# A batched x·yᵀ on one core: two heads per 128-row matmul, transposes on the vector engine, stores in 16 KB runs

## The chip, the core and the metric

The kernel runs on one NeuronCore of a Trainium2 chip. The core has a matrix engine (PE, with weight loads listed apart as PEld), a vector engine (DVE), an activation engine (ACT), a general engine (POOL) and a queue engine (SP). Sixteen DMA engines move data between the chip's DRAM and the on-chip SBUF, which has 128 partitions. Matmul results land in PSUM[...]. The metric is the device time of one execution in microseconds.

## The reference

```python
def setup_inputs():
    batch, n_heads, seq_t, seq_s, channels = 8, 12, 512, 512, 64
    # x, y: float32, (8, 12, 512, 64)

def reference(x, y):
    return np.einsum('bhtc,bhsc->bhts', x, y).astype(np.float32)
```

For each of the 96 heads, a 512x64 matrix is multiplied with the transpose of another one. The inputs are 25.17 MB together, the output is 100.66 MB, so four fifths of all bytes are stores.

## The kernel before

The 96 heads are handled in 12 groups (`NG`) of 8. A group is two halves `a` of G = 4 heads. In one half a partition holds R = 16 consecutive rows of one head (4 KB), and a head covers Q = 32 partitions. `load(g)` (L55, L56) brings y and x of a group to SBUF, one DMA of 1 MB each, in 4 KB runs, three groups ahead (`AHEAD`).

A matmul contracts over partitions, so both operands are needed with the 64 channels on partitions. `prepare(g)` makes them, as a generator that the main loop advances step by step, so that preparing the next group is spread over the matmuls of the running one. POOL casts y and x to bf16 (L73), in four instructions of 128x1024 elements. PE transposes 128x128 blocks by matmuls with an identity matrix (L82 for y, L95 for x), 32 per group, into PSUM tiles `pt`; DVE and ACT copy these to `yT` (L88, L90) and `xT` (L100, L102). Since two halves lie side by side in a block, channels of half 0 end on partitions 0 to 63 and those of half 1 on 64 to 127.

In the main loop a result tile `pm` (128 rows, two times 512 columns of fp32) is made by eight matmuls (L122), each with a weight tile of 64 rows and 32 columns, one head's 32 rows. ACT (L129) and DVE (L131) evict such tiles in turn into `ot`, which holds 32 KB per partition; `ot` has three buffers. A full `ot` is one store of 4 MB in 32 KB runs (L136). Only the first and the last half are stored in four pieces of 1 MB, in 8 KB runs (L134). All loads and stores are issued by SP on one queue; the order of the program text is the order of the queue.

Of the kernel before, what the change touches and what calls it, by code (L numbers as in the profile page):

```python
# [1 line left out]

# [5 lines left out]


@with_exitstack  # L10
def kernel(
    ctx: ExitStack,
    tc: tile.TileContext,
    x: bass.AP,
    y: bass.AP,
    out: bass.AP,
):

    nc = tc.nc
    B, H, T, C = x.shape
    _, _, S, _ = y.shape
    P = 128
    G = 4
    Q = P // G
    R = T // Q
    NG = B * H // (2 * G)  # L30
    K = R // 2
    AHEAD = 3
    fp32 = mybir.dt.float32
    bf16 = mybir.dt.bfloat16
    COPY = mybir.ActivationFunctionType.Copy
    assert C * 2 == P and S == T and R == 16

    xv = x.rearrange("b h t c -> (b h t c)").rearrange("(g a p n) -> g p a n", a=2, p=P, n=R * C)
    yv = y.rearrange("b h t c -> (b h t c)").rearrange("(g a p n) -> g p a n", a=2, p=P, n=R * C)
    ov = out.rearrange("b h t s -> (b h t s)").rearrange("(g a p n) -> g a p n", a=2, p=P, n=R * S)  # L40

    const = ctx.enter_context(tc.tile_pool(name="const", bufs=1))
    lpool = ctx.enter_context(tc.tile_pool(name="lpool", bufs=AHEAD))
    bpool = ctx.enter_context(tc.tile_pool(name="bpool", bufs=2))
    tpool = ctx.enter_context(tc.tile_pool(name="tpool", bufs=2))
    opool = ctx.enter_context(tc.tile_pool(name="opool", bufs=3))
    ptpool = ctx.enter_context(tc.tile_pool(name="ptpsum", bufs=2, space=bass.MemoryType.PSUM))
    pmpool = ctx.enter_context(tc.tile_pool(name="pmpsum", bufs=3, space=bass.MemoryType.PSUM))

    loaded = {}  # L50

    def load(g):
        xs = lpool.tile([P, 2, R, C], fp32)
        ys = lpool.tile([P, 2, R, C], fp32)
        nc.sync.dma_start(ys.rearrange("p a r c -> p a (r c)"), yv[g])  # L55
        nc.sync.dma_start(xs.rearrange("p a r c -> p a (r c)"), xv[g])  # L56
        loaded[g] = (xs, ys)

    for g in range(AHEAD):
        load(g)  # L60

    ident = const.tile([P, P], bf16)
    make_identity(nc, ident)

    def prepare(g, made):

        xs, ys = loaded.pop(g)
        yb = bpool.tile([P, R, 2, C], bf16)
        xb = bpool.tile([P, R, 2, C], bf16)
        for s, b in ((ys, yb), (xs, xb)):  # L70
            for half in range(2):
                rows = slice(half * K, (half + 1) * K)
                nc.gpsimd.tensor_copy(b[:, rows], s[:, :, rows].rearrange("p a r c -> p r a c"))  # L73
        if g + AHEAD < NG:
            load(g + AHEAD)
        yield
        yT = tpool.tile([P, G * Q, R], bf16)
        xT = tpool.tile([P, R, P], bf16)
        for half in range(2):
            pt = ptpool.tile([P, K, P], bf16)  # L80
            for k in range(K):
                nc.tensor.transpose(  # L82
                    pt[:, k, :], yb[:, half * K + k].rearrange("p a c -> p (a c)"), ident
                )
            dst = yT[:, :, half * K:(half + 1) * K]
            src = pt.rearrange("p k n -> p n k")
            if half == 0:
                nc.vector.tensor_copy(dst, src)  # L88
            else:
                nc.scalar.activation(dst, src, COPY)  # L90
            yield
        for half in range(2):
            pt = ptpool.tile([P, K, P], bf16)
            for k in range(K):
                nc.tensor.transpose(  # L95
                    pt[:, k, :], xb[:, half * K + k].rearrange("p a c -> p (a c)"), ident
                )
            dst = xT[:, half * K:(half + 1) * K]
            if half == 0:
                nc.vector.tensor_copy(dst, pt)  # L100
            else:
                nc.scalar.activation(dst, pt, COPY)  # L102
            yield
        made[g] = (xT, yT.rearrange("p n k -> p (n k)"))

    made = {}
    for _ in prepare(0, made):
        pass
    for g in range(NG):
        xT, yT = made.pop(g)  # L110
        steps = prepare(g + 1, made) if g + 1 < NG else iter(())
        for a in range(2):
            ot = opool.tile([P, R, S], fp32)
            otf = ot.rearrange("p r s -> p (r s)")
            edge = (g == 0 and a == 0) or (g == NG - 1 and a == 1)
            for k in range(K):
                if k in (0, 3, 6):
                    next(steps, None)
                pm = pmpool.tile([P, 2, S], fp32)
                for two in range(2):  # L120
                    for h in range(G):
                        nc.tensor.matmul(  # L122
                            pm[h * Q:(h + 1) * Q, two, :],
                            xT[a * C:(a + 1) * C, 2 * k + two, h * Q:(h + 1) * Q],
                            yT[a * C:(a + 1) * C, h * S:(h + 1) * S],
                            start=True, stop=True,
                        )
                if k % 2 == 0:
                    nc.scalar.activation(ot[:, 2 * k:2 * k + 2, :], pm, COPY)  # L129
                else:  # L130
                    nc.vector.tensor_copy(ot[:, 2 * k:2 * k + 2, :], pm)  # L131
                if edge and k % 2 == 1:
                    i, j = (2 * k - 2) * S, (2 * k + 2) * S
                    nc.sync.dma_start(ov[g, a][:, i:j], otf[:, i:j])  # L134
            if not edge:
                nc.sync.dma_start(ov[g, a], otf)  # L136


# [1 line left out]
_INS = ['x', 'y']  # L140
_OUTS = [((8, 12, 512, 512), 'float32')]


# [23 lines left out]
```

## Time and profile before

| | before |
|---|---|
| median of 9 runs | 307.4 us (307.31 to 307.54) |
| the profiled execution's own time | 307.42 us |
| its span, first to last instruction | 305.7 us |
| instructions in the span | 4378 |
| PE busy | 204.6 us, 1920 matmuls and 1920 weight loads |
| DVE busy | 138.6 us |
| ACT busy | 119.7 us |
| POOL busy | 49.4 us |
| DMA moved | 126.11 MB, mean 413 GB/s |
| mean granted PE clock | 0.629 of full speed |

The busy times are sums over the span and overlap. A row of the groups table reads: line, engine, operation, output <- input with shapes, count; then total busy time and mean ns of one; then the idle time just before these instructions and what ended most of it. The row "SPq ... <- ..." of the waits table reads: total wait in us, how often, longest. In the slices of the span each digit is a busy share in tenths of one fortieth of the span, here 7.6 us. In a table by stretches the share of DMA is the mean over 16 engines, and packets are booked where they start, so that a short stretch can show more than 1. The trace also has a record of every DMA packet with its start, its duration and its size, though not the engine that moved it.

### The profile page before, as it was taken

Reading aid. Unit: us, or ns where it says so; the run is one execution under the profiler, and the core shown is the slowest. Engines: PE = TensorE matmul, PEld = TensorE weight load, DVE = VectorE, ACT = ScalarE, POOL = GpSimd, SP = SyncE. Lnnn points to the kernel's source line nnn. Section 1 sums busy time; section 2 is a strip of 40 time slices with the busy share of each in tenths; the row PEclk is TensorE's granted clock in tenths of the full one; section 3 lists DMA queues with packets and bytes.
Section 4 is the critical chain, followed back from the end, with each engine's and each line's share of the span. In section 5 each row is a group of like instructions: output and inputs, shape, how many; then the busy total and the mean of one; then the engine's idle time right before and its main releaser. Section 6 shows DMA issues by size and latency. Waiting matters only on the chain.

```text
span 305.7 us, 4378 instructions
## 1 busy us (share of the span) xinstructions
PE 204.6 (67%) x1920; PEld 91.8 (30%) x1920; DVE 138.6 (45%) x120; ACT 119.7 (39%) x121; POOL 49.4 (16%) x54
## 2 busy tenths in 40 slices
PE   1899999979919928926933990991785976575000
PEld 1443234535304403502511530350251432222000
DVE  0465654657416607615633741670664664446000
ACT  1445527544423606605523441560653463325000
POOL 3754024300500500320140050041000000000000
PEclk9999999955555555755675555575575555555555
DMA  7999999999998999999999999999999999999980
GB/s 277 413 409 420 460 419 403 470 418 384 437 467 380 443 437 408 448 425 427 442 423 425 423 441 430 402 458 425 425 440 429 427 437 435 429 429 440 397 370 35
DMA packets 10867, 126.11 MB, mean 413 GB/s; under 512 B 864, under 2 KB 864, under 8 KB 7008
## 3 DMA queue, kind: packets, MB, share of 16 engines
q1 hardware_dynamic: 10848, 125.83, 97.1%
q8 instruction: 15, 0.25, 0.3%
q14 instruction: 4, 0.03, 0.0%
HBM read 25.17 MB, written 100.66 MB: 412 GB/s over the span
## 4 chain that ended last, share of the span: by engine, by line
DMA 49%; PE 29%; DVE 5%; issue 4%; ACT 3%; POOL 1%; SPq 0%; ACTq 0%
DMA out_dram<-ot 47%; PE pm L122 23%; DVE ot L131 5%; PE pt L95 4%; ACT ot L129 3%; DMA xs<-in_x_dram 2%; PE pt L82 2%; POOL xb L73 1%; ACT xT L102 0%; DVE xT L100 0%; SPq L55 0%; ACTq L129 0%; SPq L136 0%
## 5 line engine op out<-in xcount | busy, mean ns | idle before, releaser
L122 PE MATMUL pm<-yT,xT 64*32 64x512 bf16 x1536 | 160.2, 590 | 66.4 <-ACT ot L129 63.8
L131 DVE COPY ot<-pm 128x1024 f32<-128x1024 f32 x96 | 117.1, 1224 | 122.9 <-DMA out_dram<-ot 64.0
L129 ACT ACTIVATE ot<-pm 128x1024 f32<-128x1024 f32 x96 | 96.0, 1023 | 115.5 <-DMA out_dram<-ot 72.0
L122 PEld LDWEIGHTS <-xT 64*32 64x32 bf16 x1536 | 53.6, 119 | 147.8 <-issue 136.0
L73 POOL CAST yb<-ys 128x1024 bf16<-128x1024 f32 x24 | 24.3, 1042 | 143.6 <-DMA ys<-in_y_dram 68.5
L82 PE MATMUL pt<-ident,yb 128*128 128x128 bf16 x192 | 24.0, 297 | 8.6 <-POOL yb L73 6.8
L102 ACT ACTIVATE xT<-pt 128x1024 bf16<-128x1024 bf16 x12 | 12.3, 1024 | 37.0 <-PE pt L95 30.2
L95 PE MATMUL pt<-ident,xb 128*128 128x128 bf16 x192 | 25.8, 310 | 1.3 <-DVE xT L100 0.8
L73 POOL CAST xb<-xs 128x1024 bf16<-128x1024 f32 x24 | 24.3, 1042 | 13.6 <-issue 4.9
L95 PEld LDWEIGHTS <-xb 128*128 128x128 bf16 x192 | 19.4, 142 | 22.7 <-issue 20.0
L82 PEld LDWEIGHTS <-yb 128*128 128x128 bf16 x192 | 19.3, 138 | 17.8 <-issue 8.2
L88 DVE COPY yT<-pt 128x1024 bf16<-128x1024 bf16 x12 | 14.6, 1216 | 8.5 <-PE pt L82 8.5
L90 ACT ACTIVATE yT<-pt 128x1024 bf16<-128x1024 bf16 x12 | 12.2, 1019 | 8.3 <-PE pt L82 8.3
L100 DVE COPY xT<-pt 128x1024 bf16<-128x1024 bf16 x12 | 8.3, 690 | 12.2 <-PE pt L95 9.7
L90 ACT ACT_TABLE_LOAD x1 | 1.3, 1283 | 0.7 <-PEq L151 0.7
masks.py:199 POOL TENSOR_SCALAR_AFFINE_SELECT ident<-ident 128x128 bf16<-128x128 bf16 x1 | 0.3, 294 | 0.1
masks.py:197 POOL MEMSET ident<- 128x128 bf16 x1 | 0.2, 205 | 0.3 <-POOLq L151 0.3
L151 POOL MEMSET const-float32-0.0<- 128x1 f32 x1 | 0.1, 99 | 0.2 <-issue 0.2
L151 POOL MEMSET const-bfloat16-1.0<- 128x1 bf16 x1 | 0.1, 102 | 0.0
L151 POOL MEMSET const-uint8-127<- 128x1 uint8 x1 | 0.1, 102 | 0.0
L151 POOL MEMSET const-float32-1.0<- 128x1 f32 x1 | 0.1, 99 | 0.0
## 6 DMA issues: line engine op xcount, KB each, us to landing
out_dram<-ot SPq DMA_DIRECT2D x22, 4096.0 KB, 27.7
ys<-in_y_dram SPq DMA_DIRECT2D x12, 1024.0 KB, 21.0
xs<-in_x_dram SPq DMA_DIRECT2D x12, 1024.0 KB, 23.1
out_dram<-ot SPq DMA_DIRECT2D x8, 1024.0 KB, 19.1
```

The costliest lines, as they stand in the source:

```text
L73: nc.gpsimd.tensor_copy(b[:, rows], s[:, :, rows].rearrange("p a r c -> p r a c"))
L82: nc.tensor.transpose(pt[:, k, :], yb[:, half * K + k].rearrange("p a c -> p (a c)"), ident)
L88: nc.vector.tensor_copy(dst, src)
L90: nc.scalar.activation(dst, src, COPY)
L95: nc.tensor.transpose(pt[:, k, :], xb[:, half * K + k].rearrange("p a c -> p (a c)"), ident)
L100: nc.vector.tensor_copy(dst, pt)
L102: nc.scalar.activation(dst, pt, COPY)
L122: nc.tensor.matmul(pm[h * Q:(h + 1) * Q, two, :], xT[a * C:(a + 1) * C, 2 * k + two, h * Q:(h + 1) * Q], yT[a * C:(a + 1) * C, h * S:(h + ...
L129: nc.scalar.activation(ot[:, 2 * k:2 * k + 2, :], pm, COPY)
L131: nc.vector.tensor_copy(ot[:, 2 * k:2 * k + 2, :], pm)
L151: nc = _bacc.Bacc("TRN2", target_bir_lowering=False, num_devices=1)
```

## The change

The groups stay at 8 heads, but a head now covers 16 partitions with R = 32 rows each, so a load is one run of 8 KB per partition. There is no half `a` any more: a group is worked in two halves of four heads (partitions 0 to 63, and 64 to 127), and each half in two results `h` of two heads.

The transposes leave PE. POOL casts x with four instructions of 32 partitions and y with two of 64 (L70). Each moves one half of the channels (32) to other partitions. For x, the value goes into one 16-bit slot of a 32-bit word, slot `u`, on the partitions of head pair member `u`; the other slot stays zero (the tiles `zeroed` are cleared once). For y, two neighbouring rows are packed into one word. DVE then transposes 32x32 blocks of 32-bit words (L102, L107), two instructions per half of a group, straight into SBUF. The transposed x has, on 128 partitions (channel half, `u`, channel), columns in which the rows of two heads alternate; where a column belongs to the other head, the partition holds zeros.

So one matmul with a full 128x128 weight tile gives 64 rows each of two heads (L123), 384 in all. ACT evicts three of four tiles (L128) and DVE the third (L126). `ot` holds 16 KB per partition and has seven buffers; a store is 2 MB: 64 runs of 16 KB in each of two heads (L129). No store is split at the edges. The order of instructions is the program's (`manual_schedule`), with `prepare` reduced to casts at steps 0 and 1, transposes at 5 and 13, and the load of a later group at 12. For the first group, DVE and ACT share the casts.

```diff
-    G = 4
+    G = 8
...
-    NG = B * H // (2 * G)
-    K = R // 2
+    NG = B * H // G
+    K = 8
+    E = R // K
+    D = 32
...
+    ov = out.rearrange("b h t s -> (b h t s)").rearrange(
+        "(o u h q n) -> o h q u n", u=2, h=2, q=Q * E, n=K * S
+    )
...
-    bpool = ctx.enter_context(tc.tile_pool(name="bpool", bufs=2))
-    tpool = ctx.enter_context(tc.tile_pool(name="tpool", bufs=2))
-    opool = ctx.enter_context(tc.tile_pool(name="opool", bufs=3))
-    ptpool = ctx.enter_context(tc.tile_pool(name="ptpsum", bufs=2, space=bass.MemoryType.PSUM))
-    pmpool = ctx.enter_context(tc.tile_pool(name="pmpsum", bufs=3, space=bass.MemoryType.PSUM))
+    ybpool = ctx.enter_context(tc.tile_pool(name="ybpool", bufs=2))
+    tpool = ctx.enter_context(tc.tile_pool(name="tpool", bufs=4))
+    opool = ctx.enter_context(tc.tile_pool(name="opool", bufs=7))
+    pmpool = ctx.enter_context(tc.tile_pool(name="pmpsum", bufs=4, space=bass.MemoryType.PSUM))
...
+    zeroed = [const.tile([P, K * E * D], u32, name=f"xb{half}") for half in range(2)]
...
+    def casts(g, half, engines):
...
+        xb = zeroed[half]
+        xv2 = xb.bitcast(bf16).rearrange("p (k e c u) -> p k e c u", k=K, e=E, u=2)
+        base = half * 64
...
+        for ch in range(2):
+            for u in range(2):
+                lo = base + u * D
+                src = xs[lo:lo + D, :, ch * D:(ch + 1) * D]
+                cast(
+                    engines[n % len(engines)],
+                    xv2[(2 * ch + u) * D:(2 * ch + u + 1) * D, :, :, :, u],
+                    src.rearrange("p (e k) c -> p k e c", k=K),
+                )
+                n += 1
+        yb = ybpool.tile([P, R // 2 * D], u32)
+        yv2 = yb.bitcast(bf16).rearrange("p (j c w) -> p j w c", j=R // 2, w=2)
+        for ch in range(2):
+            cast(
+                engines[n % len(engines)],
+                yv2[ch * 64:(ch + 1) * 64],
+                ys[base:base + 64, :, ch * D:(ch + 1) * D].rearrange("p (j w) c -> p j w c", w=2),
+            )
+            n += 1
...
+    def transposes(g, half, xb, yb):
+        xT = tpool.tile([P, K * D * E], u32)
+        nc.vector.transpose(
+            xT.rearrange("p (k r e) -> p k e r", k=K, e=E),
+            xb.rearrange("p (k e c) -> p k e c", k=K, e=E),
+        )
+        yT = tpool.tile([P, D * R // 2], u32)
+        nc.vector.transpose(
+            yT.rearrange("p (r j) -> p j r", r=D), yb.rearrange("p (j c) -> p j c", c=D)
+        )
...
+    def result(g, half, h, steps):
...
+        ot = opool.tile([P, K, S], fp32)
+        for k in range(0, K, 2):
+            next(steps, None)
+            pm = pmpool.tile([P, 2, S], fp32)
+            for two in range(2):
+                nc.tensor.matmul(
+                    pm[:, two, :], xT[:, k + two, h, :], yT[:, h * S:(h + 1) * S], start=True, stop=True
+                )
+            if k == 4:
+                nc.vector.tensor_copy(ot[:, k:k + 2, :], pm)
+            else:
+                nc.scalar.activation(ot[:, k:k + 2, :], pm, COPY)
+        nc.sync.dma_start(ov[2 * g + half, h], ot.rearrange("p r s -> p (r s)"))
+
+    def prepare(g):
...
+        for step in range(16):
+            if step in (0, 1):
+                b[step] = casts(g, step, [nc.gpsimd])
+            if step in (5, 13):
+                transposes(g, step // 8, *b[step // 8])
+            if step == 12 and g + AHEAD < NG:
+                load(g + AHEAD)
+            yield
+
+    with tc.manual_schedule():
+        for g in range(AHEAD):
+            load(g)
+        nc.vector.memset(zeroed[0], 0.0)
+        nc.gpsimd.memset(zeroed[1], 0.0)
+        b0 = casts(0, 0, [nc.vector, nc.scalar, nc.gpsimd])
+        transposes(0, 0, *b0)
+        b1 = casts(0, 1, [nc.gpsimd, nc.scalar])
+        transposes(0, 1, *b1)
+        if AHEAD < NG:
+            load(AHEAD)
+        for g in range(NG):
+            steps = prepare(g + 1) if g + 1 < NG else iter(())
             for half in range(2):
...
+                for h in range(2):
+                    result(g, half, h, steps)
```

## The prediction

> **What bounds the kernel now.** I read the page's slices of the span first, then its table of DMA queues, then the issuing queue's waits, then busy time in chosen stretches, and last the groups of instructions. Each time below is of the one profiled execution: span 305.7 us, time 307.42 us, against a median of 307.4 us, so the two can be used for each other.
>
> ```profile
> DMA  7999999999998999999999999999999999999980
> GB/s 277 413 409 420 460 419 403 470 418 384 437 467 380 443 437 408 448 425 427 442 423 425 423 441 430 402 458 425 425 440 429 427 437 435 429 429 440 397 370 35
> ...
> q1 hardware_dynamic: 10848, 125.83, 97.1%
> q8 instruction: 15, 0.25, 0.3%
> ```
>
> The reader is to see that the 16 DMA engines are busy in every slice but the first and the last two; one queue moves all 125.83 MB in 97.1% of the engines' span. No compute engine passes 67% on the page.
>
> ```profile
> SPq L136 <- DVE ot L131: 231.8, 22, 15.2
> SPq L162 <- DMA out_dram<-ot: 22.0, 3, 17.2
> ...
> L131 DVE COPY ot<-pm 128x1024 f32<-128x1024 f32 x96 | 117.1, 1224 | 122.9 <-DMA out_dram<-ot 64.0
> L129 ACT ACTIVATE ot<-pm 128x1024 f32<-128x1024 f32 x96 | 96.0, 1023 | 115.5 <-DMA out_dram<-ot 72.0
> L73 POOL CAST xb<-xs 128x1024 bf16<-128x1024 f32 x24 | 24.3, 1042 | 13.6 <-issue 4.9
> ```
>
> SP (L136) waits for evictions, but the evictions (L129, L131) wait 72.0 and 64.0 us for stores to leave `ot`: compute is ahead and held by full buffers. At the end the program waits 22.0 us for stores alone. So a faster or slower engine is worth nothing until it falls under the DMA pace; what counts is how long the **last** DMA engine takes. Busy time by stretches (columns: length, then PE, PEld, DVE, ACT, POOL busy with counts, PE clock, DMA share, GB/s):
>
> ```profile
> 109.00:114.00 5.00, 0.00 (x0) 0.00 (x0) 0.00 (x0) 0.00 (x0) 0.00 (x0) 0.50 0.97 419
> 115.00:124.00 9.00, 8.48 (x79) 3.81 (x79) 5.91 (x6) 4.34 (x5) 0.00 (x0) 0.50 0.94 397
> 160.00:250.00 90.00, 61.38 (x588) 28.69 (x591) 43.89 (x39) 38.06 (x39) 8.11 (x8) 0.54 1.01 431
> 292.00:295.00 3.00, 0.00 (x0) 0.00 (x0) 0.00 (x0) 0.00 (x0) 0.00 (x0) 0.50 1.01 429
> 300.00:304.00 4.00, 0.00 (x0) 0.00 (x0) 0.00 (x0) 0.00 (x0) 0.00 (x0) 0.50 0.06 27
> ```
>
> The last line carries the prediction: for 4 us the DMA share is 0.06, one engine of 16, moving 27 GB/s. Fifteen engines are done and the kernel waits for one. The trace's DMA packet records (start, duration, size; no engine number) say why. A 32 KB store packet takes 1213 ns, in 2,636 of 2,816 cases exactly; 118 take 1231 to 1316 ns, 7.38 us too much in all, and they follow one another as packets of one engine do. From 109 to 114 us, with no instruction on any engine, all 52 are at 1213 or 1214 ns. From 115 to 124 us, with 173 instructions, there is one chain of slow ones (1255, 1288, 1265, 1293 ns and so on). After 282.3 us, when compute has ended, none is slow. So one DMA engine loses time while instructions run: 2,802 instructions ran during the 118 packets, 2.6 ns each. The last packet ends at 304.27 us; the other 15 engines end from 295.6 to 299.8, mean 297.6.
>
> [...]
>
> **The change, part by part.**
>
> *Packets.* Fixed sizes in the records: 4 KB 159 ns, 8 KB 309, 32 KB 1213, nearly a straight line; 16 KB lies at 309 + 8192 x (1213-309)/24576 = 610 ns. Per engine before: 384 loads x 159 + 64 edge stores x 309 + 176 stores x 1213 = 294.3 us. After: 24 loads x 8 packets x 309 = 59.3, and 48 stores x 8 x 610 = 234.2, together 293.6 us. The 18 more semaphore packets of 9 ns each are 0.2. Gain about 0.5 us.
>
> *Instructions.* 1,536 matmuls with as many weight loads and 384 transposes with theirs go; 384 matmuls with 384 loads come. PE falls from 3,840 to 768 instructions; with some 99 on DVE, 150 on ACT, 143 on POOL, 72 on SP, the program has about 1,250 against 4,378. The 15 instruction fetches (q8; 14.9 us of packets by the records, 0.9 us per engine on average) should fall to about 4: gain 0.6 us. The slow engine's loss was 304.27 - 297.6 = 6.7 us over 4,378 instructions, 1.5 ns each; at 1,250 it is 1.9 us. From the other side, 2.6 ns each gives 3.3; below, the loss can vanish, and then the others' spread (up to 2.2 us over their mean, less with fewer fetches, say 1.5) ends last. I take 1.9.
>
> *Sum.* Mean end of the engines: first packet at 1.9, 293.8 of packets, and of the 1.4 us by which 297.6 exceeded 1.9 + 294.3 the 0.8 that isn't fetches: 296.5. With 1.9 of lag, 298.4. From the last packet to the reported time were 307.42 - 304.27 = 3.15 us. That makes **301.5 us**.
>
> *Compute beside it.* A group of 8 heads has 293.6/12 = 24.5 us of DMA. In it: ACT 12 x 1.023 = 12.3 us; DVE 4 x 1.224 for evictions and two pairs of transposes. Their price is not in the trace[...]. PE: the page's matmuls of 512 columns last 590 ns on average, so 32 of them one after another are at most 18.9 us. POOL: 12 casts; the trace has 1.042 us for 128x1024, and 32 or 64 partitions with as many elements each take the same if cost goes by elements: 12.5 us. All lie under 24.5 and cost nothing; the cover is 7 `ot` tiles of 2 MB, 34 us of stores, against 3 of 4 MB. New waits: a transpose waits on POOL with DVE's evictions behind it, ACT then gets three PSUM tiles further at most before PE is held too (4 in all); this eats only into that 34 us backlog. SP's loads for three groups on stand behind three stores of the running group and wait for casts that were queued eleven steps earlier.
>
> *Start.* x lands at about 5.7 us and y at 8.2, as y and x did. ACT and POOL then have six and five casts between them, to about 12.6; transposes 1, matmuls, and ACT's three evictions put the first store at about 16. Loads of three groups fill the queue to 16.9 us and the fourth, issued at 12.6 when the casts free its tiles, to 22. No gap; with casts twice as long about 2 us of one.
>
> **Rivals.** (1) *The lag stays*: one engine is slow because evictions or stores run, not by number of instructions. For it: the slow packets come with all engines' work, which the trace can't part. Against: 2.6 ns for each instruction is steady, and PE has 88% of them. Then 296.5 + 6.7 + 3.15 = 306.3 us.
>
> (2) *POOL becomes the bound, slower than before.* The casts write every second bf16 and change partitions. [...] the 1042 ns with permuted rows speak against. It decides from 24.5/12 = 2.04 us per cast. [...]
>
> (3) *16 KB stores to two heads 1 MB x 2 apart run under the line.* 384 packets per engine: 16 ns too many on each eat the gain; at 650 ns the time is 317. Against: three sizes lie on one line.
>
> **How the numbers follow.** Forecast 0.66, own range 299.6 (no lag at all: 296.5 + 3.15) to 303.5 (3.3 us of lag and a small gap at the start). Rival 1 0.15, 305.6 to 307.4; POOL 0.08; stores 0.06; a gap of several us at the start or in the middle 0.05. The range for 8 in 10 runs from 299.4 to 306.6 and takes in most of rival 1. About 0.2%, 0.6 us, is what this kernel's measurement tells from no change: faster is below 306.8. Faster 0.66 + 0.11 + 0.04 = 0.81, same 0.05, slower 0.14.
>
> **What would show it.** Right: the stretch in which one engine works alone shrinks from about 4 us to under 2, GB/s near 428 from 20 us on, the final wait for stores ends near 300 us of span, evictions still wait for stores. Wrong: a lone engine for 4 us or more (rival 1); POOL busy over 80% and SP waiting for evictions that wait for transposes (rival 2); DMA share 9 in every slice at under 420 GB/s (rival 3). The forecast fails as soon as DMA slices drop below 9 in the middle.

## The result and the profile after

The changed kernel takes 305.0 us (median of 9 runs, 304.62 to 305.37) against 307.41 us (28 runs): a ratio of 0.9921, interval 0.9912 to 0.9929. It is faster by 2.4 us, or 0.8%, where 5.9 us were forecast. Its profiled execution took 304.83 us.

From the page of the changed kernel: span, busy times, the DMA slices, the queues, and groups.

```profile
span 303.0 us, 1551 instructions
...
PE 135.3 (45%) x384; PEld 46.2 (15%) x384; DVE 131.0 (43%) x99; ACT 144.9 (48%) x150; POOL 182.4 (60%) x142
...
DMA  7999999999999999999999999999999999999992
GB/s 294 428 376 439 415 435 424 439 421 423 438 410 427 441 416 432 435 420 432 426 433 407 430 430 423 427 433 421 425 441 425 430 426 433 428 437 425 437 428 115
...
q1 hardware_dynamic: 10368, 125.83, 98.0%
q8 instruction: 3, 0.05, 0.1%
...
L128 ACT ACTIVATE ot<-pm 128x1024 f32<-128x1024 f32 x144 | 136.8, 1028 | 120.5 <-DMA out_dram<-ot 99.8
...
L70 POOL CAST xb<-xs 32x1024 bf16<-32x1024 f32 x91 | 120.6, 1325 | 49.7 <-DMA xs<-in_x_dram 30.6
L126 DVE COPY ot<-pm 128x1024 f32<-128x1024 f32 x48 | 58.1, 1215 | 114.6 <-DMA out_dram<-ot 108.3
...
L102 DVE STREAM_TRANSPOSE xT<-xb 128x1024 uint32<-128x1024 uint32 x24 | 49.6, 2066 | 13.2 <-POOL xb L70 11.7
L107 DVE STREAM_TRANSPOSE yT<-yb 128x512 uint32<-128x512 uint32 x24 | 25.0, 1041 | 6.2 <-POOL yb L70 6.2
```

The reader is to see that nothing has changed about the bound. The DMA slices are full from the second to the last but one. Evictions, the copies of `pm` to `ot`, still wait for stores (99.8 us on ACT, 108.3 on DVE; it was 72.0 and 64.0), so compute is further ahead than before. Instructions fell from 4378 to 1551, instruction fetches (q8) from 15 to 3. Busy time by stretches of the changed kernel (columns as in the table of before):

```profile
160.00:250.00 90.00, 44.99 (x121) 14.99 (x120) 41.19 (x32) 42.88 (x46) 47.83 (x37) 0.67 1.01 427
...
294.00:296.00 2.00, 0.00 (x0) 0.00 (x0) 0.00 (x0) 0.00 (x0) 0.00 (x0) 0.50 1.01 434
296.00:298.00 2.00, 0.00 (x0) 0.00 (x0) 0.00 (x0) 0.00 (x0) 0.00 (x0) 0.50 0.40 172
298.00:300.00 2.00, 0.00 (x0) 0.00 (x0) 0.00 (x0) 0.00 (x0) 0.00 (x0) 0.50 0.27 115
300.00:302.00 2.00, 0.00 (x0) 0.00 (x0) 0.00 (x0) 0.00 (x0) 0.00 (x0) 0.50 0.04 16
```

The steady rate is as before (427 GB/s, 431 then). The end looks different. Before, one engine of 16 worked alone for 4 us; now a share of 0.27 from 298 to 300 us says that four or five engines work, and one alone only for the last 1.1 us. The trace also records when each of the 16 engines signals that its part of a DMA has landed (sixteen times for each DMA, without engine numbers). For the last store, in us from the span's start, sorted:

```
before  295.9 296.0 296.0 296.0 296.4 296.8 296.8 297.5 298.6 298.7 298.7 298.8 299.1 299.3 300.1 304.7
after   296.5 296.5 296.5 296.6 296.7 296.8 296.8 297.0 297.2 297.5 298.1 299.5 299.9 300.3 301.0 302.1
```

| last store's signals, us | before | after | forecast for after |
|---|---|---|---|
| last of 16 | 304.69 | 302.12 | 298.8 |
| mean of 16 | 298.10 | 298.07 | 296.9 |
| last over mean | 6.59 | 4.05 | 1.9 |

(The forecast counted packets' ends, which lie 0.4 us before the signal for the last one: 304.27 and 304.69 before.) So 2.5 us came from the lateness of the last engine, and nothing from the mean. Of the 3.3 us by which the profiled execution missed the forecast, 2.1 are lateness and 1.2 mean. (The forecast's mean was that of the fifteen other engines; taken so, after has a mean of 297.8 and a lateness of 4.3, and the parts are 2.4 and 0.9.)

What makes engines late in the changed kernel is read from the same signals of all DMAs: the last engine's lead over the median stands still for long and jumps at some DMAs. From 62 to 89 us it stays at 1.2 to 1.5 us and is 2.2 at 94; it goes from 3.2 to 4.3 at 170 us and from 4.4 to 5.3 at 219 us. These jumps fall on loads. (An earlier one, at 62 us, falls on one of the three instruction fetches, 0.92 us long.) The packet records agree: after 20 us, 74 of 2,156 load packets of 8 KB are more than 105 ns too long (up to 931 ns in place of 309), in bunches around the loads that stand between stores. Their excess over 309 ns sums to 22.1 us. From 5 to 20 us, where only loads run, none of 780 is. In the kernel before, the 4 KB load packets after 20 us had 8.4 us of excess.

The packet records carry no engine number, but they can be strung together by time: on one engine a packet starts 3 to 4 ns before the recorded end of the packet before it, and all 16 engines work through the same order of packet sizes. (Where two engines end within a nanosecond or two of each other, they can be taken for one another, so the sums by engine are good to some tenths of a us.) Read so, the engine that ends last in the changed kernel has 4.5 us of excess in its load packets, 0.4 us in its stores and one fetch; of the ten engines that end first, none has over 1.6 us in its loads. In the kernel before, the last engine has 7.8 us of excess in its 32 KB stores and no fetch on q8 at all.

### The profile page after: what moved, and what is told of

It reads as the page before. It is cut to its first block, busy times and chain, and to the rows that moved or that the text cites. A ratio compares the mean times of both kernels' runs of the same rounds, so it can differ in the third digit from the quotient of the medians.

```text
span 303.0 us, 1551 instructions
## 1 busy us (share of the span) xinstructions
PE 135.3 (45%) x384; PEld 46.2 (15%) x384; DVE 131.0 (43%) x99; ACT 144.9 (48%) x150; POOL 182.4 (60%) x142
## 4 chain that ended last, share of the span: by engine, by line
DMA 75%; POOL 10%; ACT 2%; issue 1%; DVE 0%; ACTq 0%; PE 0%; SPq 0%; POOLq 0%
DMA out_dram<-ot 63%; DMA ys<-in_y_dram 12%; POOL xb L70 6%; POOL yb L70 4%; ACT ot L128 2%; DVE ot L126 0%; ACTq L186 0%; PE pm L122 0%; SPq L62 0%; POOLq L70 0%; ACTq L128 0%; SPq L129 0%; DVE yT L107 0%; SPq L63 0%
## 5 line engine op out<-in xcount | busy, mean ns | idle before, releaser
L128 ACT ACTIVATE ot<-pm 128x1024 f32<-128x1024 f32 x144 | 136.8, 1028 | 120.5 <-DMA out_dram<-ot 99.8
L122 PE MATMUL pm<-yT,xT 128*128 128x512 bf16 x384 | 135.3, 504 | 131.5 <-ACT ot L128 96.7
L70 POOL CAST xb<-xs 32x1024 bf16<-32x1024 f32 x91 | 120.6, 1325 | 49.7 <-DMA xs<-in_x_dram 30.6
L126 DVE COPY ot<-pm 128x1024 f32<-128x1024 f32 x48 | 58.1, 1215 | 114.6 <-DMA out_dram<-ot 108.3
L122 PEld LDWEIGHTS <-xT 128*128 128x128 bf16 x384 | 46.2, 120 | 220.1 <-issue 194.9
L70 POOL CAST yb<-ys 64x1024 bf16<-64x1024 f32 x46 | 60.7, 1319 | 3.3 <-DMA ys<-in_y_dram 0.5
L102 DVE STREAM_TRANSPOSE xT<-xb 128x1024 uint32<-128x1024 uint32 x24 | 49.6, 2066 | 13.2 <-POOL xb L70 11.7
L107 DVE STREAM_TRANSPOSE yT<-yb 128x512 uint32<-128x512 uint32 x24 | 25.0, 1041 | 6.2 <-POOL yb L70 6.2
L68 ACT ACTIVATE xb<-xs 32x1024 bf16<-32x1024 f32 x3 | 4.0, 1348 | 0.1
L70 DVE CAST xb<-xs 32x1024 bf16<-32x1024 f32 x2 | 2.5, 1238 | 3.7 <-DMA xs<-in_x_dram 3.7
L68 ACT ACTIVATE yb<-ys 64x1024 bf16<-64x1024 f32 x2 | 2.7, 1358 | 0.0
```

What stands on the lines that cost most here:

```text
L70: engine.tensor_copy(dst, src)
L102: nc.vector.transpose(xT.rearrange("p (k r e) -> p k e r", k=K, e=E), xb.rearrange("p (k e c) -> p k e c", k=K, e=E),)
L107: nc.vector.transpose(yT.rearrange("p (r j) -> p j r", r=D), yb.rearrange("p (j c) -> p j c", c=D))
L122: nc.tensor.matmul(pm[:, two, :], xT[:, k + two, h, :], yT[:, h * S:(h + 1) * S], start=True, stop=True)
L126: nc.vector.tensor_copy(ot[:, k:k + 2, :], pm)
L128: nc.scalar.activation(ot[:, k:k + 2, :], pm, COPY)
```

## The experiments

Two theories stood after this. *Instructions*: one DMA engine loses time with each instruction; the change removed most of this loss, and what lateness is left has another cause. *Evictions or stores* (the first rival of the prediction): the lateness comes with them. And beside both, *loads*: the new transfers make engines late by themselves. "Lateness" is the last over the mean of the 16 signals of the last store; each kernel's own profiled execution gives it. That execution lies up to 0.7 us from the kernel's median, so differences in lateness that are smaller than this say little. In kernels without computing each `ot` tile is only set to zero.

**More instructions in the changed kernel.** Each matmul is cut in four, each with its own weight load; transfers and evictions are untouched.

```diff
-                nc.tensor.matmul(
-                    pm[:, two, :], xT[:, k + two, h, :], yT[:, h * S:(h + 1) * S], start=True, stop=True
-                )
+                for c in range(0, S, 128):
+                    nc.tensor.matmul(
+                        pm[:, two, c:c + 128], xT[:, k + two, h, :],
+                        yT[:, h * S + c:h * S + c + 128], start=True, stop=True,
+                    )
```

> The changed kernel with each matmul of 512 columns cut into four of 128, each with its own weight load: same work, same transfers, PE instructions 768 -> 3072, all in the program about 3850 instead of 1551. Theory 'instructions slow one DMA engine' (1.5 to 2.6 ns each, from the profile before): that engine loses 3.5 to 6 us more, slow 16 KB packets come back in one chain (some 640 ns instead of 611) whenever PE runs, and the time is 307 to 311 us. Rival 'the lag comes with evictions and stores, not with the number of instructions': 305.0 us within 0.5, few slow 16 KB packets.

It took 307.36 us (12 runs; ratio to before 0.9998, interval 0.999 to 1.0007). Page of this kernel:

```profile
span 305.4 us, 3855 instructions
...
PE 139.5 (46%) x1536; PEld 131.1 (43%) x1536; DVE 130.6 (43%) x99; ACT 144.9 (47%) x150; POOL 182.7 (60%) x142
...
q8 instruction: 12, 0.20, 0.2%
```

Its busy time by stretches, same columns:

```profile
298.00:300.00 2.00, 0.00 (x0) 0.00 (x0) 0.00 (x0) 0.00 (x0) 0.00 (x0) 0.50 0.36 156
300.00:302.00 2.00, 0.00 (x0) 0.00 (x0) 0.00 (x0) 0.00 (x0) 0.00 (x0) 0.50 0.12 49
302.00:304.00 2.00, 0.00 (x0) 0.00 (x0) 0.00 (x0) 0.00 (x0) 0.00 (x0) 0.50 0.06 25
```

The share of 0.06 is back: one engine alone from 302.7 to 304.6 us. PE's share is 46%, after 45% with the matmuls whole, so PE does not bind; the whole gain was lost with 2,304 more instructions, 2.36 us or 1.0 ns each. The engine that loses time by instructions ends 3.6 us later (304.6, after 301.0 as second last), at the lower edge of what was expected. Nine more instruction fetches of about 0.95 us came too, but none of them on this engine: strung together, its records hold no fetch on q8 and 6.9 us of excess in 16 KB stores. The rival falls, since evictions and stores are the same. The signals show the loss going on: while compute runs late in the kernel, the gap between the last and the second engine grows steadily.

```
kernel    from .. to us    gap last - second, us    instructions    ns each
before    205.0 .. 285.2   1.757 -> 4.621           1107            2.6
split     215.3 .. 275.5   0.090 -> 1.915            774            2.4
after     229.2 .. 277.8   1.792 -> 1.101            226            3.1
```

In the changed kernel the gap shrinks: there the losing engine is the second, and catches up with one that was made late by loads. That reading takes it that the same engine holds its place over these 50 to 80 us. The strung records bear it out: in these stretches the stores of that engine are 2.7, 1.7 and 0.6 us too long in sum, those of no other engine over 0.5.

**Transfers alone.** Three kernels without computing: the transfers of after, of before, and before's loads with after's stores.

```diff
-            pm = pmpool.tile([P, 2, S], fp32)
...
-        nc.sync.dma_start(ov[2 * g + half, h], ot.rearrange("p r s -> p (r s)"))
+        nc.vector.memset(ot.bitcast(u32), 0.0)
+        nc.sync.dma_start(ov[2 * g + i // 2, i % 2], ot)
```

> Leaves out all computing: the changed kernel's loads (8 KB runs) and stores (2 MB, 16 KB runs in two heads) in its order, with one clearing of each output tile in place of casts, transposes, matmuls and evictions. Some 200 instructions. Theory 'what is left of the lag in the changed kernel comes from 8 KB load packets that run beside stores': the load packets after 60 us are again some 15 to 20 us too long in sum, the last engine ends 3 to 5 us after the median, and the time is 303 to 305.5 us. Rival 'the rest of the lag too comes from instructions or computing': no long load packets, the engines end within 2 us of each other, 299.5 to 301.5 us.

> Leaves out all computing: the loads (4 KB runs) and stores (4 MB, 32 KB runs; edges in 8 KB) of the kernel before in its order, with clearings of the output tiles in place of the rest. Theory 'instructions slow one DMA engine': without them no chain of 32 KB packets at 1230 to 1316 ns, last engine at most 2 us after the median instead of 6.6, time 301 to 303 us. Rival 'one engine is slow by itself or by the stores': lag of 5 us or more, 306 to 307.5 us.

> Leaves out all computing: the loads of the kernel before (4 KB runs, two streams 512 KB apart) with the stores of the changed kernel. If the load's shape (8 KB runs[...]) makes load packets long beside stores: their excess after 60 us is under 5 us in sum, as in the kernel before, and the time is 1 to 3 us below the transfers-only run of the changed kernel. If the stores' shape (two heads 2 MB apart) makes it: excess of 15 us or more again, and a time like that run's or up to 1.8 us more (4 KB packets cost 159 against 154.5 ns per 4 KB).

| transfers alone | us | ratio to before, interval | last | mean | lateness | load excess after 20 us |
|---|---|---|---|---|---|---|
| of after | 303.65 | 0.9884, 0.9868 to 0.9901 | 300.35 | 297.46 | 2.90 | 34.0 |
| of before | 300.72 | 0.9785, 0.977 to 0.9799 | 297.68 | 296.91 | 0.77 | 18.1 |
| before's loads, after's stores | 302.15 | 0.9823, 0.9805 to 0.9841 | 299.77 | 298.10 | 1.67 | 23.0 |

Busy time by stretches without computing, transfers of before, then of after (columns: length, DVE, POOL, PE clock, DMA share, GB/s):

```profile
296.00:298.00 2.00, 0.00 (x0) 0.00 (x0) 1.00 0.21 86
298.00:300.00 2.00, 0.00 (x0) 0.00 (x0) 1.00 0.00 0
```

```profile
296.00:298.00 2.00, 0.00 (x0) 0.00 (x0) 1.00 0.23 98
298.00:300.00 2.00, 0.00 (x0) 0.00 (x0) 1.00 0.17 74
```

A share of 0.17 is three engines: in the new pattern three end at 300.3 us and thirteen by 297.4. Strung together, these three have 5.1 to 5.4 us of excess each in their load packets, the thirteen others 1.6 to 2.5: with hardly any instructions, loads alone make engines late.

This decides the case. The old transfers by themselves are done 2.9 us **earlier** than the new ones; computing then cost the old kernel 6.7 us (307.41 - 300.72) and costs the new one 1.35 (305.0 - 303.65). The change gained 5.3 us in what computing costs and gave 2.9 back in its transfers. (This takes it that the two add; they don't quite, since the loads have more excess without computing than with it.) About half of the 2.9 comes with the loads (303.65 - 302.15 = 1.5), half with the stores (302.15 - 300.72 = 1.4), each within some 0.7 us. The stores' part is mostly packet overhead that the forecast had: 384 x 611 = 234.6 us against 176 x 1213 + 64 x 309 = 233.3. In the forecast it was outweighed by the cheaper packets of the loads, a gain that the loads then didn't bring.

The excess by which the two shapes were to be told apart, after 60 us, is 16.8, 11.8 and 15.5 us in the three kernels of the table and tells nothing: the old transfers too are far over the 5 us expected. (Of the times, 300.72 lies just under the 301 to 303 us expected; the other two are as expected.)

**Loads grouped in blocks.** If engines get late where loading changes to storing, fewer changes help. `pairs` loads four groups at the start and then two at a time (5 blocks of loads instead of 9); `triples` six and then three (3 blocks). `ot` buffers make room: 6 and 4 instead of 7.

```diff
-    lpool = ctx.enter_context(tc.tile_pool(name="lpool", bufs=AHEAD))
+    lpool = ctx.enter_context(tc.tile_pool(name="lpool", bufs=AHEAD + 1))
...
-            if step == 12 and g + AHEAD < NG:
+            if step == 12 and g % 2 == 1 and g + AHEAD < NG:
                 load(g + AHEAD)
+                load(g + AHEAD + 1)
...
-        for g in range(AHEAD):
+        for g in range(AHEAD + 1):
             load(g)
...
-        if AHEAD < NG:
-            load(AHEAD)
```

> The changed kernel with the loads of two groups issued together (four load buffers, six output buffers; 4 groups at the start, then 4 times 4 MB instead of 8 times 2 MB). Theory 'the lag and the long load packets arise at the borders where some engines load and others store': half as many borders, so the lag of the last engine over the mean falls from 4.0 us to 2.5 to 3 and the time to about 303.7 us (303.2 to 304.3). Rival 'every load packet beside stores pays, however the loads are grouped': 305.0 us within 0.4; fewer output buffers cost nothing, since 29 us of stores still wait.

> Leaves out all computing: transfers as in the run of the changed kernel's transfers alone (303.65 us), but loads of two groups together. Border theory: lag over the mean 1.5 to 2 us instead of 2.9, time 302.2 to 302.9 us. Rival: 303.65 within 0.4.

> The pairs kernel with loads grouped once more: six groups at the start, then two blocks of three groups (6 MB each), six load buffers and four ot buffers. Border theory (the lag grows once for each change between loading and storing, hardly with the bytes loaded): pairs had 5 blocks of loads after or at the start and 3.15 us of lag, after had 9 and 4.05, so with 3 blocks 2.4 to 2.8 us of lag and a long-packet excess near 12 us: 303.2 to 303.6 us. Bytes theory (each load packet that runs beside stores has its chance to be long, however loads are grouped): no change against pairs, 303.8 to 304.2 us. Buffer theory (four ot buffers hold 8 MB, 20 us of stores, and a block of 6 MB of loads keeps stores back for 15 us): if that starves the DMA or compute, a gap appears in the slices and the time is 304.5 us or more.

> The transfers of the triples kernel without computing; every output tile is only set to zero, so casts, transposes, matmuls and evictions are left out and the output is zeros. Border theory: pairs went from 2.90 to 1.57 us of lag by going from 9 to 5 blocks of loads, so 3 blocks give about 0.9 us of lag and 301.6 to 302.1 us. Bytes theory: as the pairs without computing, 302.3 to 302.7 us.

| kernel | blocks | us | ratio to before, interval | last | mean | lateness | load excess |
|---|---|---|---|---|---|---|---|
| after | 9 | 305.0 | 0.9921, 0.9912 to 0.9929 | 302.12 | 298.07 | 4.05 | 22.1 |
| pairs | 5 | 303.94 | 0.9891, 0.9877 to 0.9906 | 300.87 | 297.73 | 3.15 | 17.5 |
| triples | 3 | 303.60 | 0.9872, 0.9859 to 0.9886 | 300.33 | 297.36 | 2.97 | 20.0 |
| transfers of after | 9 | 303.65 | 0.9884, 0.9868 to 0.9901 | 300.35 | 297.46 | 2.90 | 34.0 |
| transfers of pairs | 5 | 302.52 | 0.9838, 0.9826 to 0.9851 | 299.25 | 297.68 | 1.57 | 29.2 |
| transfers of triples | 3 | 301.05 | 0.9782, 0.9765 to 0.9799 | 298.83 | 296.79 | 2.04 | 18.4 |

Both beat the changed kernel and the one before; between the two the intervals overlap. Four `ot` buffers are enough, as the slices of triples show (DMA in tenths), so the buffer theory falls; below them its busy time by stretches:

```profile
DMA  7999999999999999999999999999999999999994
```

```profile
296.00:298.00 2.00, 0.00 (x0) 0.00 (x0) 0.00 (x0) 0.00 (x0) 0.00 (x0) 0.50 0.38 164
298.00:300.00 2.00, 0.00 (x0) 0.00 (x0) 0.00 (x0) 0.00 (x0) 0.00 (x0) 0.50 0.06 25
300.00:302.00 2.00, 0.00 (x0) 0.00 (x0) 0.00 (x0) 0.00 (x0) 0.00 (x0) 0.50 0.00 0
```

The transfers alone follow the blocks (1.1 us, then 1.5 us better), more than was expected of triples. With computing, the second step brings 0.3 at most, which the intervals don't tell from nothing. The lone engine in the lines above is why: in triples the gap between last and second grows from 0.238 us at 206.8 us to 1.447 at 280.9, over 433 instructions, 2.8 ns each. What the loads had hidden, the loss by instructions, is now the last thing again. The expected split was not exact, though: the load excess of triples did not fall below that of pairs (20.0 against 17.5), and without computing the step from pairs to triples is in the mean (0.9 us), while the lateness went from 1.57 to 2.04 us where 0.9 was expected. That fewer blocks save time is shown; that they do it by less lateness is shown for the first step alone.

**Size of the load packets.** Each load in two DMAs of 512 KB, in 4 KB runs, with and without computing:

```diff
-        nc.sync.dma_start(xs.rearrange("p r c -> p (r c)"), xv[g])
-        nc.sync.dma_start(ys.rearrange("p r c -> p (r c)"), yv[g])
+        for s, v in ((xs, xv), (ys, yv)):
+            for n in (0, R * C // 2):
+                nc.sync.dma_start(
+                    s.rearrange("p r c -> p (r c)")[:, n:n + R * C // 2], v[g][:, n:n + R * C // 2]
+                )
```

> The changed kernel with each load cut into two of 512 KB, in 4 KB runs. A 4 KB packet takes 159 ns, two of them 9 ns more than one of 8 KB, 1.7 us per engine over the kernel. If the size of the load packets makes the lag, the lag falls by 1.2 us or more and the time stays near 305.3 us or falls; if the addresses or the borders make it, it comes to 306.7 us.

> Leaves out all computing: the changed kernel's transfers with the loads in 4 KB runs, two DMAs for each tensor. Packet size as the cause of the lag: lag at most 1.7 us as with the loads of the kernel before, time 303 to 304 us (1.7 us of packet time added, 1.2 of lag gone). Addresses or borders as the cause: lag 2.9 again and 305 to 305.6 us.

Measured: 305.01 us with computing (ratio 0.9933, 0.992 to 0.9946) and 303.48 without (0.9875, 0.9863 to 0.9888), both as with 8 KB runs. But the parts moved: with computing the lateness falls from 4.05 to 2.79 us and the mean grows from 298.07 to 299.43; without, 2.90 to 0.89 and 297.46 to 299.39. Here the smaller load packets made engines less late, by 1.26 and 2.01 us, and cost as much in the mean, 1.36 and 1.93 us; two packets of 4 KB at 159 ns against one of 8 KB at 309 ns are 1.7 us for 192 of these on each engine, an estimate. So the lateness belongs to the size of the load packets as well as to the number of blocks; size and order of addresses change together here, and these runs don't part them.

**Instructions alone.** The transfers of before without computing, and beside them 1,552 small instructions that nothing waits for, once on ACT, once on POOL:

```diff
+    def tiny(n):
+        for _ in range(n):
+            nc.scalar.activation(dst, src, mybir.ActivationFunctionType.Copy)
...
         for c in range(4):
+            tiny(16 if (g, a, c) != (0, 0, 0) else 32)
             nc.vector.memset(ot.bitcast(u32)[:, c * 2048:(c + 1) * 2048], 0.0)
```

> The transfers of the kernel before without computing, as in the earlier run of them (300.7 us, last engine 0.8 us over the mean), and beside them 1,552 small copies of 128x64 on ACT that nothing waits for and that depend on no transfer; casts, transposes, matmuls and evictions are left out and the output is zeros. Instruction theory (one DMA engine loses 2.4 to 3.1 ns for every instruction of whatever engine, as measured late in four kernels): that engine ends 3.7 to 4.8 us later than it did, the last one 4.0 to 5.6 us over the median of the 16, and the time is 304.2 to 305.5 us. Rival, computing proper (the loss comes with matmuls, evictions or the waits between engines, not with instructions as such): lag and time stay as without the copies, 300.4 to 301.5 us. In between, 301.5 to 303.5: only some instructions count, or fetches of instructions alone (about 5 of 0.95 us spread over engines).

> The same with 1,552 small memsets of 128x64 on POOL in place of the copies on ACT; casts, transposes, matmuls and evictions are left out and the output is zeros. Instruction theory: the same as on ACT, 304.2 to 305.5 us, whichever engine runs them. Rival, computing proper: 300.4 to 301.5 us. If ACT's and POOL's instructions differ by over 1 us, it is not the number of instructions but the engine that issues them.

The times say nothing: 450.97 us and 326.59 us, because the small instructions themselves last longer than the transfers (a group of each page, ACT then POOL):

```profile
L54 ACT ACTIVATE dst<-src 128x64 f32<-128x64 f32 x1552 | 397.6, 256 | 48.8
```

```profile
L54 POOL MEMSET dst<- 128x64 uint32 x1552 | 234.4, 151 | 89.2 <-POOLq L89 0.3
```

The expectations had not reckoned with that. The signals of the last store still answer:

```
extra on   ends of the last store, 16 engines                                          instructions to 298 us
nothing    296.4 296.5 296.5 296.5 296.6 296.6 ... 297.2 297.2 297.3 297.6 297.7         227
ACT        295.9 295.9 295.9 295.9 295.9 295.9 ... 296.1 296.3 296.7 299.9 301.3        1251
POOL       295.7 295.8 295.8 295.8 295.8 295.8 ... 296.1 296.3 296.4 301.1 302.7        1647
```

Fourteen engines end earlier than without the extra work, two end 4 to 7 us after the median engine. The last end moves by 3.65 us for 1,024 more instructions and by 4.99 us for 1,420, but these two numbers give no price of an instruction. Neither kernel fetches instructions on queue q8, but both do on q14, in packets of 8 KB; both pages have the same line, and without the extra work it counts 2:

```profile
q14 instruction: 14, 0.11, 0.1%
```

Ten of these packets (ACT) and thirteen (POOL), mostly of 0.31 us, start before 298 us. Strung together, eight of the ten and ten of the thirteen lie on the engine that ends last, so a good part of its delay is fetching. The second last engine has only one of them, and there the 32 KB stores are 2.9 us (ACT) and 3.9 us (POOL) too long in sum, while without the extra work no engine has over 0.6. That is 2.3 ns for each of the 1,251 instructions and 2.4 ns for each of the 1,647, at the lower end of the 2.4 to 3.1 expected. So neither matmuls, evictions nor waits between engines are needed: copies on ACT and memsets on POOL alone slow one of the 16 DMA engines, and the fetches that many instructions bring hold up another one.

## Why the prediction was right about the bound and wrong about the gain

**What bounds the kernel**: right. The last DMA engine sets the end in every kernel run here, but for the two whose small instructions outlast the transfers.

**Packets**: the 16 KB packet, interpolated at 610 ns, takes 611; the new store shape uses all 16 engines (16 signals for each of the 48 stores). The step that failed first is "24 loads x 8 packets x 309": right for loads among loads, wrong for those beside stores, whose delay was put at nothing. Their excess after 20 us is 22.1 us over 16 engines, 1.4 us each, where the kernel before had 8.4 us, 0.5 each. That is 0.86 us of the 1.2 by which the mean of the engines was missed. For the rest there are two candidates, 384 store packets that take 1 ns more each (0.4 us) and the dip of the DMA share at 20 to 24 us shown below (0.6 us by an estimate from these shares); no run parts them.

**Instructions**: the mechanism was right and is now shown by itself (cut matmuls 2.4 ns each late in the kernel, copies on ACT 2.3, memsets on POOL 2.4). The lag, "I take 1.9", is the step that failed by more: it measured 4.05 us. What failed in it above all is "the others' spread (up to 2.2 us over their mean, less with fewer fetches, say 1.5)", the lateness that other engines would have if the loss by instructions fell away. An engine made late by loads ends last, at 302.1, with 4.5 us of excess in its load packets, and without any computing three such engines end at 300.3. The loads' packets thus failed twice, in the mean and in the lag.

The loss by instructions, "at 1,250 it is 1.9 us", was probably too small too; by how much is open. The count is one reason: the span has 1,551 instructions, and the 320 that wait on semaphores or control the program were left out. The price may be the other: 1.5 ns is the average since the start, where the same records gave 2.6 for the stretch in which the loss could be seen by itself. 2.6 x 1,551 is 4.0 us, and the losing engine, the second last, ends 3.9 us over the median (301.0 - 297.1); but that they agree is in part chance, since only 1.7 us of excess lie in its stores, and the 2.6 us in its loads are more than any of the ten first engines has (1.6). A reading was off a little as well: 297.6 us, for the mean end of the other fifteen engines before, is that of their landing signals, set beside a packet's end of 304.27; by strung packets it is 297.3.

**From the last packet to the reported time**: right; from the last signal on it is 2.71 us (304.83 - 302.12) after 2.73 before.

**Compute beside it**: right in the sum, off in the price of a cast. A cast takes 1325 ns instead of 1042, so POOL has 8 x 1.325 + 4 x 1.319 = 15.9 us in a group of 24.5, below the 2.04 us per cast at which it would decide. The x transpose takes 2066 ns and the y transpose 1041, which no run had shown before this one; DVE has 4 x 1.215 + 2 x (2.066 + 1.041) = 11.1 us in a group. Beside these evictions a pair of transposes could last (24.5 - 4 x 1.215) / 2 = 9.8 us, an estimate, before DVE would decide. All of it stays hidden, as the longer waits for stores show.

**Start**: the first store is issued at 16.62 us (about 16 forecast), the fourth load of x at 12.40 (12.6). "No gap" is not quite right; stretches of the changed kernel, columns as above:

```profile
20.00:22.00 2.00, 0.59 (x2) 0.19 (x2) 1.27 (x2) 2.00 (x3) 1.88 (x3) 1.00 0.86 336
22.00:24.00 2.00, 0.09 (x1) 0.08 (x1) 2.00 (x3) 0.09 (x1) 1.96 (x2) 0.98 0.83 344
```

The last load before the first store lands about 0.8 us late: the median of its signals comes at 23.5 us, 3.3 us after the load before it, where the step was 2.5 us until then. Without computing it comes at 23.5 us as well, so this is the first change from loads to stores and no wait for casts.

**Rivals**: the first, that the lag stays, gave 306.3, not far from 305.0, by luck: its reason, evictions or stores, fell with the cut matmuls, and the lag that stayed is of another engine. POOL as the bound and slow 16 KB stores both fell, by 1325 ns and 611 ns. The rival that was missing is the one that came: transfers that are worse by themselves, 2.9 us.

**The sign to watch** was met and misled: an engine alone for under 2 us. It is alone for 1.1 us, and yet five engines end between 299.5 and 302.1. The sign should have been the mean and the last of the 16.

## What to carry to other kernels

In a kernel bound by DMA, read the end of each of the 16 engines, not the mean rate: fewer instructions can shorten the last engine's path even where compute is hidden: here 2,304 matmuls and weight loads more cost 2.36 us, while evictions waited 105.5 us (ACT) and 113.3 us (DVE) for stores. Before changing the shapes of transfers, run both sets of transfers with no computing: here that run alone would have shown that the new ones are 2.9 us worse and the old ones had 6.7 us to win. Bring loads in few large blocks where buffers allow it: here that was worth 1.1 us with 5 blocks and 1.4 us with 3.

## What the runs showed of the hardware that was not expected

- Instructions on PE, ACT or POOL cost mainly one of the 16 DMA engines time, seen in its store packets: 2.3 to 3.1 ns each where this stood by itself, 1.0 ns each in the whole time of the kernel with cut matmuls. Why is open: every execution timed here was also recorded, and the recording itself may be what costs; no run parts the two.
- Instruction fetches on q14 (8 KB, mostly 0.31 us) can gather on one DMA engine: ten of thirteen beside the POOL memsets.
- An 8 KB load packet takes 309 ns among loads, and up to 931 ns in the changed kernel where loads and stores change over. Without computing the excess was larger (34.0 us) than with it (22.1), but not after 60 us (16.8 and 17.7); three engines had 5.1 to 5.4 us of it each.
- A POOL cast of 32x1024 elements that writes every second 16-bit slot takes 1325 ns, the dense one of 128x1024 took 1042.
- A DVE transpose of 32-bit words takes 2066 ns for 1024 and 1041 ns for 512 words per partition, about 2 ns a word.
